# Averaging windows of 16: GpSimd folds the second row of each tile before VectorE sums it

## The chip, the cores and the metric

The kernel runs on one core of one Trainium2 chip. The metric is the device time of one execution in microseconds (us). The kernel before takes 333.82 us, the median of three runs (333.63 to 333.95).

## The reference

The input is 32 x 256 rows of 4096 floats. Each row is cut into 256 windows of 16, and the output holds the mean of each window.

```python
batch, channels, length = 32, 256, 4096
output_size = 256
for i in range(output_size):
    start = int(i * length / output_size)
    end = int((i + 1) * length / output_size)
    result[:, :, i] = np.mean(x[:, :, start:end], axis=-1)
```

134.2 MB are read and 8.4 MB written, all in float32. Each input element is used once.

## The kernel before

The 8192 rows are put on 128 partitions, and each tile holds R = 2 rows per partition: 8192 floats, which are 512 windows (`cells`) of 16. There are 32 tiles in one loop, written out. The first 28 tiles (`head`) take their rows from `x_many`, in which each partition owns 56 consecutive rows, and leave their results in the SBUF tensor `res_many`. The last 4 tiles (`tail`) take theirs from `x_few`, 8 rows per partition, and leave them in `res_few`.

A tile goes through three steps. SyncE issues its load of 4 MB into `xin`, a pool tile with four buffers (L72). VectorE sums each window, 8192 elements into 512 (L75). ScalarE multiplies the 512 sums by 1/16, in place in the result tensor (L76). The results of the first 28 tiles go out in one store of 7 MB, and those of the last 4 in one store of 1 MB. Both go through the helper at L59.

All loads and both stores are issued by SyncE and go through one DMA queue in program order. The load of tile t + 4 waits until VectorE has read the buffer of tile t. The large store is issued behind the load of the last tile, and the small one after ScalarE's last operation. The framework sets the waits between engines from what each instruction reads and writes. Only the two stores have a semaphore of their own, `stored`, which SyncE waits for at the end (L87). Nothing else orders the engines against each other. GpSimd has no work in the loop; it sets four constants at the start.

Of the kernel before, what the change touches and what calls it, by code (L numbers as in the profile page):

```python
# [1 line left out]

# [4 lines left out]


@with_exitstack
def kernel(  # L10
    ctx: ExitStack,
    tc: tile.TileContext,
    x: bass.AP,
    output_size: int,
    out: bass.AP,
):

    nc = tc.nc
    F32 = mybir.dt.float32
    X = mybir.AxisListType.X

    batch, channels, length = x.shape
    ob, oc, olen = out.shape
    assert ob == batch and oc == channels and olen == output_size
    assert length % output_size == 0
    window = length // output_size  # L30
    inv_w = 1.0 / float(window)

    P = nc.NUM_PARTITIONS
    R = 2
    tail = 4
    rows = batch * channels
    assert rows % (P * R) == 0
    ntiles = rows // (P * R)
    head = ntiles - tail
    many = head * R  # L40
    few = tail * R
    cells = R * output_size
    cols = R * length

    xr = x.rearrange("b c l -> (b c) l")
    orow = out.rearrange("b c o -> (b c) o")
    x_many = xr[0 : P * many, :].rearrange("(p r) l -> p (r l)", p=P, r=many)
    o_many = orow[0 : P * many, :].rearrange("(p r) o -> p (r o)", p=P, r=many)
    x_few = xr[P * many :, :].rearrange("(p r) l -> p (r l)", p=P, r=few)
    o_few = orow[P * many :, :].rearrange("(p r) o -> p (r o)", p=P, r=few)  # L50

    res_many = nc.alloc_sbuf_tensor("res_many", [P, head * cells], F32, align_bytes=256)
    res_few = nc.alloc_sbuf_tensor("res_few", [P, tail * cells], F32, align_bytes=256)
    inpool = ctx.enter_context(tc.tile_pool(name="inpool", bufs=4))

    stored = nc.alloc_semaphore("stored")

    def store(out, in_):
        ins = nc.sync.dma_start(out=out, in_=in_)  # L59
        tc.no_tile_sem_insts.add(ins.ins.name)  # L60
        ins.then_inc(stored, 16)

    for t in range(ntiles):
        k = t - head
        xin = inpool.tile([P, cells, window], F32, name="xin")
        if k < 0:
            res, base = res_many, t * cells
            src = x_many[:, t * cols : (t + 1) * cols]
        else:
            res, base = res_few, k * cells  # L70
            src = x_few[:, k * cols : (k + 1) * cols]
        nc.sync.dma_start(out=xin.rearrange("p o w -> p (o w)"), in_=src)  # L72
        if t == ntiles - 1:
            store(o_many, res_many[:, :])
        nc.vector.reduce_sum(out=res[:, base : base + cells], in_=xin[:, :, :], axis=X)  # L75
        nc.scalar.mul(  # L76
            out=res[:, base : base + cells],
            in_=res[:, base : base + cells],
            mul=inv_w,
        )  # L80
    store(o_few, res_few[:, :])

    ctx.pop_all().close()
    tc.close()
    tc.compile()
    nc.sync.wait_ge(stored, 32)
    nc.sync.sem_clear(stored)  # L87


# [1 line left out]
_INS = ['x', 'output_size']  # L91
_OUTS = [((32, 256, 256), 'float32')]

_NUMBERS = {'output_size': 256}


# [26 lines left out]
```

## Time and profile before

| | |
|---|---|
| median of three runs | 333.82 us |
| the profiled execution, its own time | 333.91 us |
| its span, first to last instruction | 332.6 us |
| VectorE busy | 278.0 us, 32 instructions |
| ScalarE busy | 21.4 us, 33 instructions |
| GpSimd busy | 0.2 us, 4 instructions |
| HBM read, written | 134.22 MB, 8.39 MB |
| mean rate over the span | 429 GB/s |

The profile is of one execution. Busy times are of the engines' instructions; issuing a DMA does not count as busy. The page cuts the span into 40 slices of 8.3 us. In the rows of the engines and of the DMA each digit is the busy share of a slice in tenths, and the row GB/s is what the DMA moved. A group of instructions is shown by line, engine, operation, output and input with their shapes, and count; then the busy time and the mean ns of one; then the idle time of the engine before them and what ended it. DVE is VectorE, ACT is ScalarE, POOL is GpSimd, SPq is SyncE's queue of instructions. The chain of waits goes back from the last instruction to what released it, step by step. An issue of a DMA is shown with its size and with the median time from issue to landing.

DMA traffic is recorded by packets when they are complete. A stretch shorter than a few packets can therefore read over 100% or as empty.

### The profile page before, as it was taken

How to read it: one execution, taken by the hardware profiler on the slowest of the kernel's cores; microseconds unless marked ns; L12 is line 12 of the kernel's file. 1: busy time of each engine (PE TensorE's matmuls, PEld its weight loads, DVE VectorE, ACT ScalarE, POOL GpSimd, SP SyncE). 2: the span in 40 equal slices, each digit the busy share in tenths (PEclk: the TensorE clock that was granted, in tenths of full speed). 3: DMA queues.
4: the chain of work that ended last, by engine and by line, in shares of the span. 5: the costliest groups of instructions: out<-in, count | busy, mean ns of one | idle time of the engine just before them, and what ended most of it. 6: DMA issues, size and time to landing. Idle time of an engine off the chain costs nothing.

```text
span 332.6 us, 173 instructions
## 1 busy us (share of the span) xinstructions
DVE 278.0 (84%) x32; ACT 21.4 (6%) x33; POOL 0.2 (0%) x4
## 2 busy tenths in 40 slices
DVE  0488998888899888889988888998888889888870
ACT  1000000000000000000000000000000000000000
POOL 0000000000000000000000000000000000000000
DMA  8999999999999999999999999999999999999998
GB/s 315 441 441 441 441 434 410 418 441 441 441 441 437 418 410 437 441 441 441 437 426 402 437 441 441 441 441 434 418 410 441 441 441 441 437 430 418 449 441 347
DMA packets 4896, 142.61 MB, mean 429 GB/s; under 512 B 544, under 2 KB 544, under 8 KB 544
## 3 DMA queue, kind: packets, MB, share of 16 engines
q1 hardware_dynamic: 4896, 142.61, 99.5%
HBM read 134.22 MB, written 8.39 MB: 429 GB/s over the span
## 4 chain that ended last, share of the span: by engine, by line
DMA 75%; DVE 21%; SPq 0%; ACT 0%; issue 0%
DMA xin<-in_x_dram 75%; DVE res_many L75 18%; DVE res_few L75 3%; SPq L72 0%; ACT res_few L76 0%
## 5 line engine op out<-in xcount | busy, mean ns | idle before, releaser
L75 DVE TENSOR_REDUCE res_many<-xin 128x512 f32<-128x8192 f32 x28 | 243.2, 8686 | 39.9 <-DMA xin<-in_x_dram 39.9
L75 DVE TENSOR_REDUCE res_few<-xin 128x512 f32<-128x8192 f32 x4 | 34.7, 8686 | 4.0 <-DMA xin<-in_x_dram 4.0
L76 ACT ACTIVATE res_many<-res_many 128x512 f32<-128x512 f32 x28 | 17.6, 629 | 264.2 <-DVE res_many L75 264.2
L76 ACT ACTIVATE res_few<-res_few 128x512 f32<-128x512 f32 x4 | 2.5, 630 | 36.2 <-DVE res_few L75 36.2
L76 ACT ACT_TABLE_LOAD x1 | 1.3, 1283 | 0.7 <-PEq L104 0.7
L104 POOL MEMSET const-bfloat16-1.0<- 128x1 bf16 x1 | 0.1, 102 | 0.0
L104 POOL MEMSET const-uint8-127<- 128x1 uint8 x1 | 0.1, 102 | 0.0
L104 POOL MEMSET const-float32-0.0<- 128x1 f32 x1 | 0.1, 99 | 0.2 <-issue 0.2
L104 POOL MEMSET const-float32-1.0<- 128x1 f32 x1 | 0.1, 99 | 0.0
## 6 DMA issues: line engine op xcount, KB each, us to landing
xin<-in_x_dram SPq DMA_DIRECT2D x32, 4096.0 KB, 30.0
out_dram<-res_many SPq DMA_DIRECT2D x1, 7168.0 KB, 46.3
out_dram<-res_few SPq DMA_DIRECT2D x1, 1024.0 KB, 10.0
```

The source lines that it names most:

```text
L75: nc.vector.reduce_sum(out=res[:, base : base + cells], in_=xin[:, :, :], axis=X)
L76: nc.scalar.mul(out=res[:, base : base + cells], in_=res[:, base : base + cells], mul=inv_w,)
L104: nc = _bacc.Bacc("TRN2", target_bir_lowering=False, num_devices=1)
```

## The change

In each tile GpSimd first adds, in the second row of each partition (windows `m` to `cells`), the last eight elements of each window onto the first eight, in place in `xin`. VectorE's one reduction becomes two: the first row whole, 4096 elements into 256 sums, and the second row folded, 2048 elements into 256 sums, read as runs of 8 with a distance of 16. ScalarE's multiplication, the loads and the stores are as before. The order in the program is GpSimd's addition, the reduction of the first row, the reduction of the second.

```diff
@@ -28,6 +28,7 @@
     window = length // output_size
+    hw = window // 2
     inv_w = 1.0 / float(window)
@@ -40,6 +41,7 @@
     cells = R * output_size
+    m = cells // 2
     cols = R * length
@@ -72,7 +74,17 @@
-        nc.vector.reduce_sum(out=res[:, base : base + cells], in_=xin[:, :, :], axis=X)
+        nc.gpsimd.tensor_add(
+            out=xin[:, m:cells, 0:hw],
+            in0=xin[:, m:cells, 0:hw],
+            in1=xin[:, m:cells, hw:window],
+        )
+        nc.vector.reduce_sum(
+            out=res[:, base : base + m], in_=xin[:, 0:m, :], axis=X
+        )
+        nc.vector.reduce_sum(
+            out=res[:, base + m : base + cells], in_=xin[:, m:cells, 0:hw], axis=X
+        )
         nc.scalar.mul(
             out=res[:, base : base + cells],
             in_=res[:, base : base + cells],
```

## The prediction

> **What bounds the kernel now.** I read the page from the top. The forty slices and the queue rows come first, because they say whether any engine can matter at all.
>
> ```profile
> span 332.6 us, 173 instructions
> DVE 278.0 (84%) x32; ACT 21.4 (6%) x33; POOL 0.2 (0%) x4
> DVE  0488998888899888889988888998888889888870
> DMA  8999999999999999999999999999999999999998
> GB/s 315 441 441 441 441 434 410 418 441 441 441 441 437 418 410 437 441 441 441 437 426 402 437 441 441 441 441 434 418 410 441 441 441 441 437 430 418 449 441 347
> q1 hardware_dynamic: 4896, 142.61, 99.5%
> ```
>
> VectorE (DVE) is 84% busy, but the row of the DMA engines is full from the first slice to the last, also in the first and the last slice, where VectorE does little or nothing. One queue carries everything, and its packets fill 99.5% of the span. The groups of instructions agree: VectorE has to wait for data before every tile.
>
> ```profile
> L75 DVE TENSOR_REDUCE res_many<-xin 128x512 f32<-128x8192 f32 x28 | 243.2, 8686 | 39.9 <-DMA xin<-in_x_dram 39.9
> L76 ACT ACTIVATE res_many<-res_many 128x512 f32<-128x512 f32 x28 | 17.6, 629 | 264.2 <-DVE res_many L75 264.2
> L76 ACT ACTIVATE res_few<-res_few 128x512 f32<-128x512 f32 x4 | 2.5, 630 | 36.2 <-DVE res_few L75 36.2
> ```
>
> The timeline of VectorE gives the beat. The first reduction starts at 12.73 us, the last at 313.21: (313.21 - 12.73) / 31 = 9.69 us a tile, against 8.69 us of work. A tile is 128 x 8192 x 4 bytes = 4.194 MB, so the beat is 433 GB/s.
>
> The end needs care. The chain of waits runs through the last reduction and the last ScalarE operation, which reads as if 8.7 us of VectorE stood bare behind the last load:
>
> ```profile
> 313.18 0.02 issue
> 313.21 8.70 DVE res_few L75
> 321.93 0.63 ACT res_few L76
> ```
>
> The issues of the two stores say otherwise:
>
> ```profile
> out_dram<-res_many SPq DMA_DIRECT2D x1, 7168.0 KB, 46.3
> out_dram<-res_few SPq DMA_DIRECT2D x1, 1024.0 KB, 10.0
> ```
>
> By the timeline the large store is issued at 283.85 us, behind the load of the last tile in the same queue, and lands at 283.85 + 46.3 = 330.1. The small one is issued at 322.58 and needs 10.0 us to land, at 332.6. Alone, 1.049 MB would take 1.049 / 0.433 = 2.4 us, plus what a first transfer needs to get going: the first load takes 12.0 us from issue to landing, 2.3 us over its 9.69. So 4.7 us, and the other 5.3 are waiting behind the large store. The sum of bytes closes on this: after 313.2 us there are 8.39 MB of stores left, 8.39 / 0.433 = 19.4 us, and 313.2 + 19.4 = 332.6, the span. The kernel is bound by bytes through one queue up to its last microsecond, and the tail of VectorE and ScalarE lies under the large store with 5.3 us to spare.
>
> **The change, part by part.**
>
> *VectorE.* Removed: 32 reductions of 8192 elements, 8.69 us each. Added: 32 of 4096 and 32 of 2048. In proportion that is 4.34 and 2.17 us. How much of 8.69 is a fixed cost isn't in this trace, which has one size only. ScalarE's whole operation on 512 elements, 0.63 us, is my upper bound for a fixed cost, and with it (8.69 - 0.63) / 8192 an element, the two come to 4.66 and 2.64 us. I take 4.4 and 2.2, near the proportion, since a reduction of 8.69 us can hide little that is fixed: 6.6 us a tile (6.5 to 7.3).
>
> *GpSimd.* Added: 32 additions of 2048 pairs in place, in runs of 8 elements. The trace shows GpSimd only in four memsets of one element per partition, 0.10 us each. Lower bound: one pair in the time of one of VectorE's elements, 1.06 ns, so 2.2 us. Reading both operands one after the other, 4096 elements, gives 4.3 us at VectorE's pace and 5.0 at ScalarE's (0.63 us / 512). If the write took its turn too, 6144 elements at ScalarE's pace are 7.6 us. The far upper bound is that each of the 256 runs costs as much as a memset, 256 x 0.10 = 26 us. I take 4.7 us, by the elementwise rows, which are nearer in kind than a memset of one element.
>
> For the same number of pairs the Trainium skill (GPSIMD Engine Reference, section Elementwise — side-by-side cycle accounting) states 4497 ns measured; no run here shows it yet.
>
> *The wait that is added.* The second reduction waits for GpSimd. GpSimd and the first reduction both start when the tile lands, so the wait is 4.7 - 4.4 = 0.3 us, and a tile is through VectorE 4.7 + 2.2 + 0.1 for handovers = 7.0 us after landing, 1.7 us earlier than now. Behind the waiting instruction on VectorE stands only the first reduction of the next tile, whose data come 9.69 us after this tile's. ScalarE (L76) and the sync queue (L72, the load into the freed buffer) wait for the second reduction.
>
> *Does an earlier or later release matter?* Four buffers: when tile t is released, the queue still holds 1.0 us of tile t+1, and tiles t+2 and t+3, 20.4 us of work in all. With 2.3 us for a transfer to get going, a release may come 18 us later before the queue runs dry, and an earlier one only lets the load wait longer. GpSimd's first instruction may take some us more than the others: it falls into the same cover. Cost nothing. If the cover went, each us past 18 would cost about a us a tile.
>
> *The engines' beat.* Each must stay under 9.69 us a tile: VectorE 6.6 plus 0.3 of wait, GpSimd 4.7, ScalarE 0.63 as before. All do. GpSimd would have to be twice as slow as I take it to set the beat.
>
> *The tail.* The last tile lands at 313.2; VectorE ends at 320.2 and the small store is issued at 320.9 instead of 322.58. It still stands behind the large store until 330.1 and ends at 332.6. The stall does not go; it moves into the queue, and the time to landing grows from 10.0 to about 11.7 us.
>
> *The queue.* No DMA is added, removed or put in another order. Whether its rate suffers from GpSimd reading and writing the buffers is not in the trace. VectorE's reading costs it nothing: the large store's packets of 57 KB land every 2.1 us both while VectorE works (314.5 to 321) and when it rests (323 to 329), by half-microsecond windows. I take 0 for GpSimd; a gain is excluded, since VectorE's reading, which shrinks, costs nothing now.
>
> Sum: 332.6 us of span with no term changed, plus the 1.3 us that lie around it in the profiled execution, **333.9 us**. That execution took 333.91; the median of the three runs is 333.82, 0.03% less, well inside what the forecast can claim.
>
> One rule of the Trainium skill speaks against the change: Perfetto Trace Analysis, section Optimizing Scalar/DVE Operations, says that GpSimd shares an SBUF read port with VectorE, so that moving work between those two might not help. SBUF — State Buffer, section Who interferes with whom, narrows it: a reduction of VectorE on trn2 never contends. By the first the serial rival below would come true, by the second not; no run here shows it yet.
>
> **The rivals.**
>
> *One at a time (slower).* If GpSimd and VectorE can't work on the buffers together, a tile costs 4.4 + 2.2 + 4.7 = 11.3 us, over 9.69, and the engines set the beat. First landing 12.7, 32 x 11.3 = 361.6, ScalarE 0.6, then the small store alone 4.7, and 1.3 around the span: 381 us, 14% slower. It decides from a sum over 9.69 us. For it: nothing in the trace. Against it: only that the sum must be fully serial; half an overlap (9.0) would be hidden. 4%.
>
> *GpSimd sets the beat (slower).* Over 9.69 us for one addition. At 12 us it is 12.7 + 384 + 2.2 + 0.6 + 4.7 + 1.3 = 405 us, at the 26 of the far bound 853. Against it: even two reads and a write in turn at ScalarE's pace stay at 7.6. 4%.
>
> *The queue slows under GpSimd's traffic (slower).* 0.1 us a tile, 1% of the beat, is 32 x 0.1 = 3.2 us: 337.1 us. It decides from 0.02 us a tile. For it: per tile the engines touch 12288 elements a partition instead of 8192. Against it: the steady packets above. 8%.
>
> *The tail counts (faster).* If the end hung on VectorE as the chain has it, 1.7 us would go: 332.2 us, 0.5% faster. Against it: the bytes, which account for the whole end. 5%.
>
> *It doesn't do what it says.* If the first reduction were made to wait for GpSimd because both touch one buffer, a tile would be through 11.4 us after landing; VectorE still works 6.6 of 9.69, release is 2.7 us later of 18, the small store goes out at 325.3, before 322.58 + 5.3 = 327.9. The time is the forecast's, and it is counted there.
>
> **How the numbers follow.** A measurement of this kernel can tell about 0.2% (0.67 us) from no change. Forecast 79% (333.2 to 334.6); slower 4 + 4 + 8 = 16%; faster 5%. The forecast's own interval holds a little under 8 in 10, so the range goes up into the slowed queue, half of its price: 333.1 to 335.5. The two cases of a new beat lie outside, and with them the far bound of GpSimd's addition; the bounds of the reductions cost nothing inside it.
>
> **What would show it.** DMA full in all slices and 99.5% for the queue; the first reductions still 9.69 us apart; reductions of about 4.4 and 2.2 us, a GpSimd addition of about 4.7, and more idle time of VectorE before the first reduction; the small store issued near 321 and still landing at 332.6, its 10.0 us grown to 11 or 12. I am wrong if the beat moves off 9.69 us (then see whether GpSimd's instructions fill it, or stretch VectorE's, or the packets themselves take longer), or if the end comes less than 19 us after the last landing.

## The result, and the profile after

The changed kernel takes 334.53 us, the median of 19 runs (334.22 to 334.68), beside 333.81 us for the kernel before (19 runs, 333.63 to 334.13). The ratio is 1.002, with a 95% interval of 1.0013 to 1.0027. It is 0.7 us slower, a small loss that is real, since no run of the one lies among the runs of the other. The profiled execution took 334.62 us with a span of 333.3.

The page of the changed kernel, its span, busy times, DMA row and queues (packets, MB, share of 16 engines):

```profile
span 333.3 us, 267 instructions
DVE 214.6 (64%) x64; ACT 21.4 (6%) x33; POOL 142.7 (43%) x36
...
DMA  8999999999999999999999999999999999999998
...
q1 hardware_dynamic: 4896, 142.61, 99.4%
q14 instruction: 2, 0.02, 0.0%
```

VectorE has lost 63 us of work and the span has grown. The DMA row is as full as before. The last line is new: during the span two packets of a second queue, named instruction, passed through the same DMA engines. On the page of before there is no such line. The packet records reach back to 11 us before the span, and there six packets of 8 KB pass on this queue in both kernels. What is new is that two more come while the 16 engines are full.

Its groups of instructions and its DMA issues (KB each, us to landing):

```profile
L77 POOL TENSOR_TENSOR xin<-xin 128x2048 f32<-128x2048 f32 x32 | 142.5, 4452 | 175.6 <-DMA xin<-in_x_dram 175.6
L82 DVE TENSOR_REDUCE res_many<-xin 128x256 f32<-128x4096 f32 x28 | 123.8, 4420 | 89.7 <-DMA xin<-in_x_dram 89.7
L85 DVE TENSOR_REDUCE res_many<-xin 128x256 f32<-128x2048 f32 x28 | 64.0, 2286 | 4.7 <-POOL xin L77 4.2
...
xin<-in_x_dram SPq DMA_DIRECT2D x32, 4096.0 KB, 31.8
out_dram<-res_many SPq DMA_DIRECT2D x1, 7168.0 KB, 48.0
out_dram<-res_few SPq DMA_DIRECT2D x1, 1024.0 KB, 11.8
```

The three new instructions have nearly the lengths that were forecast, and the second reduction waits 0.17 us for GpSimd. The loads take 1.8 us longer from issue to landing than before (30.0), and so does the small store (10.0): everything that VectorE hands back earlier waits longer in the queue.

Where do the 0.7 us come in? The timeline of VectorE shows it (start us, us, idle before):

```profile
216.43 4.42 DVE L82 TENSOR_REDUCE res_many<-xin 128x256 f32<-128x4096 f32 x1 [2.76 <-DMA xin<-in_x_dram]
...
226.11 4.42 DVE L82 TENSOR_REDUCE res_many<-xin 128x256 f32<-128x4096 f32 x1 [2.80 <-DMA xin<-in_x_dram]
...
236.59 4.42 DVE L82 TENSOR_REDUCE res_many<-xin 128x256 f32<-128x4096 f32 x1 [3.60 <-DMA xin<-in_x_dram]
...
246.26 4.42 DVE L82 TENSOR_REDUCE res_many<-xin 128x256 f32<-128x4096 f32 x1 [2.79 <-DMA xin<-in_x_dram]
```

In the kernel before, the same two tiles are 9.74 us apart:

```profile
226.02 8.69 DVE L75 TENSOR_REDUCE res_many<-xin 128x512 f32<-128x8192 f32 x1 [0.99 <-DMA xin<-in_x_dram]
235.76 8.69 DVE L75 TENSOR_REDUCE res_many<-xin 128x512 f32<-128x8192 f32 x1 [1.05 <-DMA xin<-in_x_dram]
```

Tile after tile lands at a distance of 9.68 us, as before; the median step is 9.68 us in both kernels. One single step, from 226.11 to 236.59, is 10.48, and it is the only one over 9.8. The packet records of the trace have one of the two instruction packets there: 8192 bytes, from 230.43 us, 0.31 us long. The load packet that follows it takes 1.74 us instead of the usual 1.21. Together that is 0.31 + 0.53 = 0.84 us on one of the 16 DMA engines.

The delay is never made good. Each load ends with 16 packets of 4 bytes. They are read here as one for each DMA engine, which the trace doesn't number: how far the 16 lie from their median hardly changes from one load to the next. At the load before the instruction packet (the 23rd) the last of the 16 is 0.26 us behind the median. At the next one, a single packet is 0.90 us behind and the other 15 no more than 0.26. At the end of the run the last is still 0.87 us behind. In the kernel before, it is 0.29 us at the same load and 0.30 at the end. So one DMA engine fell behind there and stayed behind, which makes 0.57 us of the difference between the two profiled executions. The rest lies in the median of the 16, which ends 0.17 us later and is 0.13 us later from the first load on, before either packet. At the end the last two data packets, 0.31 us apart, are complete at 332.61 and 332.92 us, and all others by 332.41; in the kernel before the last one of all is complete at 332.18.

**Theory:** the longer streams of instructions make the loading of code visible: an 8 KB packet stands in one DMA engine, that engine is late from there on, and the kernel ends with its slowest DMA engine. **Rival:** GpSimd's reading and writing of the buffers slows the transfers. **A second rival:** each added instruction costs a little.

### The profile page after: what moved, and what is told of

The parts are those of the page before. It is cut to its first block, busy times and chain, and to the rows that moved or that the text cites. A ratio compares the mean times of both kernels' runs of the same rounds, so it can differ in the third digit from the quotient of the medians.

```text
span 333.3 us, 267 instructions
## 1 busy us (share of the span) xinstructions
DVE 214.6 (64%) x64; ACT 21.4 (6%) x33; POOL 142.7 (43%) x36
## 4 chain that ended last, share of the span: by engine, by line
DMA 79%; POOL 9%; DVE 6%; POOLq 1%; issue 0%; SPq 0%; ACT 0%
DMA xin<-in_x_dram 79%; POOL xin L77 9%; DVE res_many L85 5%; POOLq L97 1%; DVE res_few L85 1%; SPq L74 0%; ACT res_few L88 0%; POOLq L77 0%
## 5 line engine op out<-in xcount | busy, mean ns | idle before, releaser
L77 POOL TENSOR_TENSOR xin<-xin 128x2048 f32<-128x2048 f32 x32 | 142.5, 4452 | 175.6 <-DMA xin<-in_x_dram 175.6
L82 DVE TENSOR_REDUCE res_many<-xin 128x256 f32<-128x4096 f32 x28 | 123.8, 4420 | 89.7 <-DMA xin<-in_x_dram 89.7
L85 DVE TENSOR_REDUCE res_many<-xin 128x256 f32<-128x2048 f32 x28 | 64.0, 2286 | 4.7 <-POOL xin L77 4.2
L82 DVE TENSOR_REDUCE res_few<-xin 128x256 f32<-128x4096 f32 x4 | 17.7, 4420 | 11.2 <-DMA xin<-in_x_dram 11.2
L85 DVE TENSOR_REDUCE res_few<-xin 128x256 f32<-128x2048 f32 x4 | 9.1, 2286 | 0.7 <-POOL xin L77 0.7
## 6 DMA issues: line engine op xcount, KB each, us to landing
out_dram<-res_few SPq DMA_DIRECT2D x1, 1024.0 KB, 11.8
```

What stands on the lines that cost most here:

```text
L77: nc.gpsimd.tensor_add(out=xin[:, m:cells, 0:hw], in0=xin[:, m:cells, 0:hw], in1=xin[:, m:cells, hw:window],)
L82: nc.vector.reduce_sum(out=res[:, base : base + m], in_=xin[:, 0:m, :], axis=X)
L85: nc.vector.reduce_sum(out=res[:, base + m : base + cells], in_=xin[:, m:cells, 0:hw], axis=X)
```

## The experiments

All were timed in 5 rounds with the kernel before on the same chip; its medians there were 333.74 us (E1 to E4), 333.80 (E5 to E8) and 333.75 (E9 to E11). Streams are counted in the compiled program, all of an engine's instructions; the kernel before has 40 on VectorE, 18 on GpSimd, 41 on ScalarE, the changed one 72, 79 and 41. "Around" is the profiled execution's time less its span. The packet times are the starts of the 8 KB instruction packets in the trace, from the span's start; those ahead of the span, six in most kernels and seven in E5, E7, E8 and E11, are left out. Where the text says "by the completions", it means the 16 packets at the end of each load, read as above.

| run | VectorE, GpSimd, ScalarE | packets at us | median us | less before | around us |
|---|---|---|---|---|---|
| before | 40, 18, 41 | none | 333.81 | | 1.33 |
| changed | 72, 79, 41 | 230.4, 308.9 | 334.53 | +0.72 | 1.32 |
| E1 split alone | 72, 18, 41 | 230.2 | 334.41 | +0.67 | 1.34 |
| E2 GpSimd to scratch | 40, 82, 41 | 297.7 | 334.09 | +0.35 | 1.33 |
| E3 GpSimd folds both rows | 72, 79, 41 | 307.5, 307.6 | 334.47 | +0.73 | 1.32 |
| E4 ScalarE in four | 40, 18, 137 | 122.5; 334.0 after the span | 334.17 | +0.43 | 1.36 |
| E5 every fourth tile | 48, 34, 41 | none | 333.80 | 0.00 | 1.33 |
| E6 ScalarE in eight | 40, 18, 265 | 74.1, 229.5; 334.6 after the span | 334.69 | +0.89 | 1.45 |
| E7 first 20 tiles | 60, 55, 41 | 334.0 after the span | 334.19 | +0.39 | 1.72 |
| E8 GpSimd in every second tile | 40, 50, 41 | none | 333.78 | -0.02 | 1.33 |
| E9 split of 20 tiles | 60, 18, 41 | 334.1 after the span | 334.28 | +0.53 | 1.90 |
| E10 split of 26 tiles | 66, 18, 41 | 329.3 | 334.45 | +0.70 | 1.34 |
| E11 both rows, every second tile | 56, 49, 41 | 334.1 after the span | 334.23 | +0.48 | 1.67 |

**E1: VectorE's split without GpSimd.**

```diff
-        nc.vector.reduce_sum(out=res[:, base : base + cells], in_=xin[:, :, :], axis=X)
+        nc.vector.reduce_sum(
+            out=res[:, base : base + m], in_=xin[:, 0:m, :], axis=X
+        )
+        nc.vector.reduce_sum(
+            out=res[:, base + m : base + cells], in_=xin[:, m:cells, :], axis=X
+        )
```

> GpSimd gets no work; VectorE sums each tile in two reductions of 4096 elements, so its stream has as many instructions as in the changed kernel (72 instead of 40). Theory (code loading: a longer instruction stream makes one or two 8 KB instruction packets pass through the DMA engines during the run, and the engine that carries one ends about 0.7 us late): if the packet at 230 us is VectorE's, one such packet appears and the time is 0.5 to 0.8 us over the kernel before, near 334.5. Rival (GpSimd's traffic slows the queue): no GpSimd work, so the time of the kernel before, 333.8, and no packet matters.

334.41 us, ratio 1.0018 (1.0010 to 1.0027). The queues on its page, and VectorE's timeline:

```profile
q14 instruction: 1, 0.01, 0.0%
```

```profile
225.83 4.42 DVE L77 TENSOR_REDUCE res_many<-xin 128x256 f32<-128x4096 f32 x1 [0.94 <-DMA xin<-in_x_dram]
230.17 4.41 DVE L80 TENSOR_REDUCE res_many<-xin 128x256 f32<-128x4096 f32 x1
236.38 4.42 DVE L77 TENSOR_REDUCE res_many<-xin 128x256 f32<-128x4096 f32 x1 [1.80 <-DMA xin<-in_x_dram]
```

With GpSimd idle, nearly the whole surplus is there, with one packet, and the same long step at the same tile: 10.55 us from 225.83 to 236.38. By the completions one DMA engine is 0.92 us behind the median from that tile to the end, where the last was 0.17 behind at the tile before. The rival of GpSimd's traffic can't explain that. The packet at 230 us is VectorE's.

**E2: GpSimd's additions without VectorE's split.** The sums are those of the kernel before; what GpSimd adds is not used.

```diff
+    scr = nc.alloc_sbuf_tensor("scr", [P, m * hw], F32, align_bytes=256)
...
+        nc.gpsimd.tensor_add(
+            out=scr[:, :].rearrange("p (o w) -> p o w", w=hw),
+            in0=xin[:, m:cells, 0:hw],
+            in1=xin[:, m:cells, hw:window],
+        )
         nc.vector.reduce_sum(out=res[:, base : base + cells], in_=xin[:, :, :], axis=X)
```

> VectorE as in the kernel before, one reduction of a whole tile. GpSimd makes the same additions, but writes them to a scratch tensor that nobody reads, so its stream is as long as in the changed kernel (82 instructions instead of 18) and VectorE's is not. Theory of code loading: if one of the two packets is GpSimd's, one 8 KB packet appears during the run and the time is 0.3 to 0.8 us over the kernel before. If both were VectorE's: no packet and 333.8. Rival (GpSimd's traffic): 334.5 with or without a packet, and a beat over 9.69 us.

334.09 us, ratio 1.0011 (1.0002 to 1.0020), with one packet late in the run. The profiled execution itself took 333.89, the least of the 11, and has hardly a surplus to look at: its only step over 9.8 us is 9.85, at the packet. By the completions one DMA engine goes there from about 0.2 us ahead of the median to 0.32 behind it, hardly later than the last one was already (0.28). So what a packet costs at the end depends on the engine that it meets. Over the 11 runs the surplus lies in the span, 332.7 us by the median beside 332.4 for the kernel before on this chip. The groups of its page:

```profile
L83 DVE TENSOR_REDUCE res_many<-xin 128x512 f32<-128x8192 f32 x28 | 243.2, 8686 | 39.8 <-DMA xin<-in_x_dram 39.8
L78 POOL TENSOR_TENSOR scr<-xin 128x2048 f32<-128x2048 f32 x32 | 142.4, 4451 | 174.9 <-DMA xin<-in_x_dram 174.9
```

VectorE's reduction takes 8686 ns beside GpSimd's addition, the same as without it. The mean step of the landings is 9.69 us, as before. The surplus alone does not say whether it is the packet or the traffic; E8 does.

**E3: twice the traffic, streams as long as in the changed kernel.** VectorE has one reduction a tile here; in the place of the second one stands a wait for GpSimd.

```diff
+        nc.gpsimd.tensor_add(
+            out=xin[:, :, 0:hw],
+            in0=xin[:, :, 0:hw],
+            in1=xin[:, :, hw:window],
+        )
+        nc.vector.reduce_sum(
+            out=res[:, base : base + cells], in_=xin[:, :, 0:hw], axis=X
+        )
```

> GpSimd folds both rows of each tile in one addition of 4096 pairs, about 8.8 us, and VectorE has one reduction of 4096 elements. Both streams are as long as in the changed kernel; GpSimd's traffic and time are doubled. Theory of code loading: two packets and the time of the changed kernel, 334.5. Rival (traffic): the surplus doubles, 335.2. A GpSimd addition over 9.69 us would set the beat and give far more.

334.47 us, ratio 1.0021 (1.0012 to 1.0030): the surplus of the changed kernel, not twice it. GpSimd needs 8722 ns a tile, 90% of the beat, and the median step of the landings is still 9.68 us. Its two packets come at 307.5 and 307.6 us, so close that their times overlap. By the completions two DMA engines are 0.60 and 0.74 us behind the median after them, where none was more than 0.11 behind, and the surplus is that of one. The issues of its page show how little of the tail's cover was left:

```profile
xin<-in_x_dram SPq DMA_DIRECT2D x32, 4096.0 KB, 25.4
out_dram<-res_many SPq DMA_DIRECT2D x1, 7168.0 KB, 42.4
out_dram<-res_few SPq DMA_DIRECT2D x1, 1024.0 KB, 5.4
```

**E4: a longer stream on an engine that the change doesn't touch.**

```diff
-        nc.scalar.mul(
-            out=res[:, base : base + cells],
-            in_=res[:, base : base + cells],
-            mul=inv_w,
-        )
+        for j in range(4):
+            a = base + j * (cells // 4)
+            b = a + cells // 4
+            nc.scalar.mul(out=res[:, a:b], in_=res[:, a:b], mul=inv_w)
```

> The kernel before, with ScalarE's multiplication of each tile cut into four, so that ScalarE's stream grows from 41 to 137 instructions; GpSimd without work, VectorE as before. ScalarE has some 9 us of slack a tile. Theory of code loading: one or two 8 KB packets during the run, 334.3 to 334.7. Rival (GpSimd's traffic): 333.8.

334.17 us, ratio 1.0013 (1.0004 to 1.0021), by the median a little under the expected 334.3 to 334.7. One packet passes at 122.5 us, and the step of the landings there is 10.15 us, the only one over 9.8:

```profile
119.38 8.69 DVE L75 TENSOR_REDUCE res_many<-xin 128x512 f32<-128x8192 f32 x1 [1.01 <-DMA xin<-in_x_dram]
129.53 8.69 DVE L75 TENSOR_REDUCE res_many<-xin 128x512 f32<-128x8192 f32 x1 [1.46 <-DMA xin<-in_x_dram]
```

ScalarE is busy 9% of the span, and still its instructions cost time: not by being executed, but by being loaded.

**E5: the change in every fourth tile.** The loop takes the changed body where `t % 4 == 3` and that of before elsewhere.

> The change in every fourth tile only (8 of 32): GpSimd folds the second row there and VectorE sums in two reductions; the other tiles are as in the kernel before. VectorE's stream has 48 instructions, GpSimd's 34. Theory (code loading decides): VectorE's packet came with its 45th reduction or so, and here there are 40, so no packet passes during the run and the time is that of the kernel before, 333.75. Rival (each split or fold costs a little): a quarter of the surplus of 0.7, so 333.9.

333.80 us, ratio 0.9999 (0.9991 to 1.0008). No packet during the span, no surplus; a quarter of it would have been 333.98 by this chip's base, which the median speaks against and the interval alone would not. The queues have one line only on the page, which shows the span alone:

```profile
q1 hardware_dynamic: 4896, 142.61, 99.6%
```

**E8: GpSimd's traffic without its packet in the span.** The sums are those of before; GpSimd's are not used. `n` is 480 of the 512 windows.

```diff
+        if t % 2 == 1:
+            nc.gpsimd.tensor_add(
+                out=scr[:, :].rearrange("p (o w) -> p o w", w=hw),
+                in0=xin[:, 0:n, 0:hw],
+                in1=xin[:, 0:n, hw:window],
+            )
```

> VectorE as in the kernel before. In every second tile GpSimd adds 3840 pairs of it into a scratch tensor that nobody reads: 15/16 of the additions of the run in which GpSimd wrote to a scratch in every tile, in half the instructions (GpSimd's stream 50 instead of 82). Theory: its packet does not pass, and the time is that of the kernel before, 333.75. Rival (GpSimd's traffic costs that run its 0.35 us): 334.07.

333.78 us, ratio 1.0000 (0.9991 to 1.0009). The page:

```profile
DVE 277.9 (84%) x32; ACT 21.4 (6%) x33; POOL 131.2 (39%) x20
...
q1 hardware_dynamic: 4896, 142.61, 99.6%
```

GpSimd is busy 131.2 us, against 142.7 in the changed kernel, and the kernel's median is that of before. The rival's time on this chip, 333.80 + 0.33 = 334.13, lies over all 11 runs (333.65 to 334.07), and no run's span is over 332.5 us. The rival of the traffic falls with E8, and the packet is what is left for the 0.35 us of E2. The longer stream does load more code: seven packets of 8 KB pass before the span instead of six, where the kernel's own transfers haven't begun (the first starts at 1.7 us), and no time is lost. One thing stays open: in three of the 11 runs 1.64 to 1.77 us lie around the span, and the trace is of a run with 1.33.

**E6: two packets.** As E4, with 8 in the place of 4.

> As the run with ScalarE's multiplication cut into four, but cut into eight: ScalarE's stream grows to 265 instructions. There the first packet passed at 122 us and a second one 128 instructions later, after the end. Here the first is due near 68 us and a second near 223 us. If both go through the same DMA engine, its delays add up and the time is near 334.6; if through different ones, the end has the larger of the two delays alone and the time is 334.2, as with one. If packets were not the cause but the number of instructions, it would be twice the surplus of 0.43, 334.6, without two long steps of the landings.

334.69 us, ratio 1.0026 (1.0016 to 1.0036). Two packets pass at 74.1 and 229.5 us, 155 us apart, which are 16 tiles of eight multiplications, 128 instructions. VectorE's timeline around both:

```profile
70.91 8.69 DVE L75 TENSOR_REDUCE res_many<-xin 128x512 f32<-128x8192 f32 x1 [0.99 <-DMA xin<-in_x_dram]
81.14 8.69 DVE L75 TENSOR_REDUCE res_many<-xin 128x512 f32<-128x8192 f32 x1 [1.54 <-DMA xin<-in_x_dram]
...
226.22 8.69 DVE L75 TENSOR_REDUCE res_many<-xin 128x512 f32<-128x8192 f32 x1 [0.99 <-DMA xin<-in_x_dram]
236.59 8.69 DVE L75 TENSOR_REDUCE res_many<-xin 128x512 f32<-128x8192 f32 x1 [1.68 <-DMA xin<-in_x_dram]
```

Two steps of 10.23 and 10.37 us among steps of 9.67, and the surplus is twice that of E4 (0.89 against 0.43; in both a small part lies around the span, with the packet after its end). Both packets are ScalarE's, and by the completions both meet the same DMA engine: the last of the 16 is 0.54 us behind the median after the first packet, 0.40 just before the second and 0.96 after it, and the other 15 are then no more than 0.14 behind. So their delays add up, whereas E3's, in two DMA engines, did not. The expectation's reading of E4, a second packet 128 instructions after the first, doesn't hold: after 122.5 us only 84 multiplications were left there.

**E7, E9, E10: where in a stream the packet comes.** E7 has the change in the first 20 tiles, E9 E1's split in the first 20, E10 E1's split in the first 26; the other tiles are as in the kernel before.

> The change in the first 20 tiles only; VectorE's stream has 60 instructions with 52 reductions, GpSimd's 55. Theory: the packet belongs to a place in VectorE's stream. In the changed kernel it came with the 45th reduction (tile 22, at 230 us); here the 45th belongs to tile 24, so one packet passes near 250 us, the step of landings there is 0.8 us longer, and the time is that of the split alone, 334.4. GpSimd's stream stays short of its packet. Rival (each split or fold costs a little): 20/32 of 0.7, so 334.2, and no single long step; if the packet belonged to a time, it would stay at 230 us.

> GpSimd without work; VectorE sums the first 20 tiles in two reductions each and the rest in one, so its stream has 60 instructions, as in the run that had the change in the first 20 tiles. There no packet passed during the span, one passed after it, and the time around the span was 1.72 us instead of 1.33. If that late packet is VectorE's: the same here, no packet in the span, 1.7 us around it, 334.2. If it was GpSimd's: nothing, 333.8. If each split costs a little: 20/32 of the split's 0.67, 334.2 too, but inside the span.

> As before with the first 26 tiles in two reductions: VectorE's stream has 66 instructions with 58 reductions. If the packet of 230 us belongs to a fixed place in the stream, the 45th reduction, and only needs a stream that goes on far enough: a packet near 230 us again and 334.4. If it belongs to a fixed distance from the stream's end (19 reductions before it): near 39 reductions, about 200 us, and 334.4. If the stream is still short of it: as with 60 instructions.

E7 was a miss: no packet near 250 us, no long step, and the span is 332.4 us, no longer than before. The time is there all the same, 334.19 us, ratio 1.0012 (1.0003 to 1.0021), because 1.72 us lie around the span instead of 1.33, and one packet comes after its end. By its number this is also the rival's 334.2; what speaks against a cost of each split is that the spans of the 11 runs are no longer than before (332.4 us by the median). E9 shows that this late packet is VectorE's: with GpSimd idle it is there again, with 1.90 us around the span and 334.28 us, ratio 1.0015 (1.0006 to 1.0024). E10 was a miss too: its packet came at 329.3 us, neither at 230 nor at 200, beside the packets of 57 KB of the large store, and the time is 334.45 us, ratio 1.0017 (1.0009 to 1.0026). With 48 instructions there is none, with 56 and 60 one after the span, with 66 one at its end, with 72 one at 230 us. So a fixed place in the stream is refuted, and so is a fixed distance from its end. What sets the moment stays open. That a packet after the span is what lengthens the time around it is not shown either: in E4 and E6 one comes there too, and the time around the span is 1.36 and 1.45 us.

**E11: the same offload in half the instructions.** In even tiles the body of E3, in odd ones that of before.

> The change's offload in half the instructions: in every second tile GpSimd folds both rows in one addition and VectorE sums them in one reduction of 4096 elements; the other tiles are as in the kernel before, the last one too. GpSimd makes the same number of additions as in the changed kernel, and VectorE is relieved of as many elements; VectorE's stream has 56 instructions instead of 72, GpSimd's 49 instead of 79. Theory: both streams stay short of their packets in the span, the time is that of the kernel before, 333.8 (334.2 if VectorE's late packet comes with 56 already as it did with 60). Rival (the offload itself costs something): 334.5.

334.23 us, ratio 1.0015 (1.0006 to 1.0024). The page and the issues:

```profile
span 332.6 us, 222 instructions
DVE 208.2 (63%) x32; ACT 21.4 (6%) x33; POOL 139.7 (42%) x20
...
out_dram<-res_few SPq DMA_DIRECT2D x1, 1024.0 KB, 6.5
```

Inside the span the offload is free: 332.6 us, as before, with VectorE relieved of 70 us. Around it lie 1.67 us, with the late packet, as the expectation's second case had it. No version gained on the kernel before, and in all of them the queue's packets fill 99.3% of the span or more.

The second rival, a little for each added instruction, doesn't fit. GpSimd's stream is 32 instructions longer in E8, at no cost, and in the changed kernel, E1, E4 and E6 the time inside the span comes in one or two long steps at VectorE's and ScalarE's packets, while the median step stays at 9.67 or 9.68 us. Only the time around the span, in E7, E9 and E11, has no such step to show for it.

## Why the prediction was right, and the step that failed

*The bound* held. VectorE's work fell by 63 us without any gain, and the 1.8 us that the tail gave up (1.7 forecast) went into the queue: the small store was issued 7.6 us after the last landing instead of 9.4, and its time to landing grew from 10.0 to 11.8 us, near the 11.7 forecast. In E3, with the tail longer than before, it fell to 5.4 us, still under the large store. The rival in which the tail counts is refuted by both.

*The sizes* were right within 6%: 4.42 and 2.29 us for the reductions (4.4 and 2.2), 4.45 for GpSimd (4.7). The wait was 0.17 us instead of 0.3. A tile is through VectorE 6.9 us after landing (7.0).

*One at a time* is refuted: the reduction of 4096 elements takes 4420 ns with GpSimd at work beside it and 4420 in E1 without. Here the Trainium skill's SBUF — State Buffer (Who interferes with whom), by which such a reduction doesn't contend, agrees with the runs, and the caution in Perfetto Trace Analysis (Optimizing Scalar/DVE Operations) doesn't come true. *GpSimd sets the beat* is refuted too, and even 8.72 us an addition stays hidden.

*The queue* is the step that failed: "No DMA is added, removed or put in another order." Two were added during the span, which no line of the kernel issues: the packets that load code. The price that the prediction gave a slower queue, 0.1 us in every tile by GpSimd's traffic, has the wrong cause and the wrong shape. The traffic costs nothing (E8), and the time comes in one step of 0.8 us in one tile. That bytes through full DMA engines set the time was right; it was applied to the kernel's own transfers alone.

The time, 334.53 us, lies in the forecast's own interval at its upper edge; the surplus of 0.72 us is just over the 0.67 that was called no change. It fits by its smallness: the forecast had no term for it, and the room that the range leaves above was meant for the traffic.

The Trainium skill (Runtime: NRT & Kernel Launch, Instruction fetch mechanics) has engines refill their instruction memory by DMA and calls the cost of crossing a block mostly hidden. For the compute engine that holds here: VectorE waited for the tile's data, and had 2.8 us to spare in the steps around. For the DMA engine, which had none, it doesn't, and the measured 0.35 to 0.7 us for a packet decide.

## What to carry to other kernels

Where the DMA row is full from end to end, relieving an engine gives nothing: sum the bytes that are left after the last landing before believing a chain that ends on an engine. There, count the instructions too. In these runs engines with time to spare took work for nothing only as long as their streams loaded no more code during the span or after it. An instruction line in the page's queues, together with one long step in the landings, is the sign of it. It can be missing: E7, E9 and E11 lost 0.39 to 0.53 us with neither, and there the time less the span shows it.

## What the runs showed of the hardware

- Code loading shows as packets of 8 KB on a queue of its own, 0.31 us each during the span, and delays one DMA engine by 0.5 to 0.8 us, since the load packet behind it is longer as well (1.43 to 1.75 us instead of 1.21). At the end 0.35 to 0.7 us of it are left for one packet, and 0.89 for two through the same DMA engine (E6, 0.12 of it around the span).
- Where VectorE's packet comes after the span (E7, E9, E11), the time around the span is 1.67 to 1.90 us instead of 1.33; where ScalarE's does (E4, E6), it is 1.36 and 1.45. Packets before the span, six or seven, cost nothing that these runs show.
- VectorE's reduction has 1.04 ns an element and a fixed 0.15 us, from 8686, 4420 and 2286 ns for 8192, 4096 and 2048 elements. Runs of 8 elements at a distance of 16 cost no more than whole rows: 4420 ns in E3 and in E1.
- GpSimd's addition has 2.08 ns a pair and a fixed 0.18 us, from 4452 and 8722 ns for 2048 and 4096 pairs.
